# An encoder layer on one Trainium2 core: attention numerators turned, pattern weights through DRAM, pattern sums on GpSimd

## Chip, cores and metric

The kernel runs on one core of one Trainium2 chip. The metric is the device time of one execution in microseconds (us), lower is better. A difference of about 0.2% (5.6 us) is the smallest that a measurement of this kernel tells from no change.

## What is computed

One layer over 2048 tokens of width 1024, in float32: RMSNorm, one input projection to 4096 columns, a mixer of 8 attention heads (64 wide) beside 4 bidirectional HGRN2 heads (128 wide), an output projection with residual, then a mixture of 16 experts that each pick 256 tokens. The part that matters here is the attention:

```
for window, dilation in ((128, 1), (512, 4), (2048, 16)):     # three patterns
    m, den, num = dilated_window_attention(qh, kh, vh, window, dilation, slopes)
scale  = exp(m_all - max over patterns of m_all)
numer  = sum over patterns of scale * num                      # (S, heads, 64)
denom  = sum over patterns of scale * den
a_out  = numer / denom
x      = x + concat(a_out, hgrn_out) @ W_out
```

## The kernel before

The program is laid out by a scheduler that works with priorities: `first`, `feed`, `mixer`, `fill` are lanes, from most to least urgent, and the order on each engine is fixed when the program is built. The input projection runs as 16 units (`project`), each 8 token groups of 48 matmuls with 256 columns (L234 to L236); each weight is used as a high and a low half. Its weights come in 8 pieces (`prep`): a load into the ring `wraw` (5 buffers, L163, L166), then ScalarE makes the high half `whi` (L168) and VectorE the low half `wlo` (L169), both in rings of 11. So of the next unit's 8 pieces 3 can be made early, and 5 wait raw in `wraw`. The HGRN2 heads run in lane `mixer` beside the projections, then the 8 attention heads (`heads`, `att_head`) beside the last projections and beside half 1 of the output projection (`op_mm`, L799 to L801, HGRN columns), whose matmuls are in lane `fill`. After the heads `op_tile` does half 0 of the output projection (attention columns), the second norm and the router for 16 tiles of 128 tokens; then comes the routing search and the experts.

A head goes over four token groups g of 512. `four(pat, ...)` handles four units of 128 queries of one pattern in one or two `block`s. In a block TensorE forms the scores (L650, L651), VectorE adds the bias table and takes the minimum (L662, the scores are negated), ScalarE takes the exponential (L663), TensorE turns the result in four 128x128 transposes (L665), VectorE or ScalarE copies it to `eT` (L667, L669), and the numerator matmul (L674) has `eT` as the stationary operand, 128 columns wide, and the values as the moving one: 64 columns and a column of ones, which gives the denominator. float32 matmuls run as two passes, so each has two records in the trace. There are 8 x (32 + 32 + 16) = 640 numerator matmuls. Pattern 2 runs whole in g = 0. Numerators, denominators and minima (66 numbers a token) of patterns 0 and 2 go through DRAM (`num_d`, L698, L719, L726) into the token order of pattern 1. There VectorE makes the three weights (L732 to L738), scales (L739) and sums (L741, twice), and the result goes to `mix_d` in token rows (L742). `op_mm` reads a tile of `mix_d`, turns it on TensorE (L788), splits it in a high and a low half (L791, L792) and multiplies.

SyncE issues nearly all transfers from one queue, in order. GpSimd copies queries (`queries`, L621, L624), doubles keys (L547) and clears borders of `ex` (L653, L655).

Of the kernel before, what the change touches and what calls it, by code (L numbers as in the profile page):

```python
# [45 lines left out]
def encoder_layer(ctx, tc, x, norm1_w, w_in, q_norm_w, k_norm_w, lb_f, lb_b, o_norm_w, w_out,  # L46
# [26 lines left out]
    num_d = scratch("num_d", (2, 8, S, 66))  # L73
    mix_d = scratch("mix_d", (S, D))
# [86 lines left out]
    def prep(cols, kc):  # L161

        raw = ring.tile([128, 2, 128], F32, name="wraw", bufs=5)  # L163
# [8 lines left out]
    def evac_qk(u):  # L172

        def f(g, p):
# [5 lines left out]
            sq = ring.tile([128, 2, 256], F32, name="asq", bufs=1)  # L180
# [130 lines left out]
    def hg_head(p, T, h):  # L311
# [57 lines left out]
        for g in range(4):  # L369
# [125 lines left out]
            sp.dma_start(dram_ap(mix_d, a * D + 512 + h * 128, [[D, 128], [128 * D, 4], [1, 128]]), o)  # L495


    def att_setup(p):
        T = {}
        dl = p.tile([128, 512], F32, name="ex", bufs=4)  # L500
# [14 lines left out]
        T["wq"], T["wk"] = wq, wk  # L515
# [6 lines left out]

        T["vp"] = [p.tile([128, n, 65], F32, name=f"vp{i}", bufs=1) for i, n in enumerate((17, 20, 16))]
        for vp in T["vp"]:
            dve.memset(vp[:, :, 64:65], 1.0)

        for vp, n, step in ((T["vp"][0], 17, 16), (T["vp"][1], 20, 1)):
            for b in range(0, n, step):
                if step > 1 or b % 5 in (0, 4):
                    dve.memset(vp[:, b, :64], 0.0)  # L530
# [61 lines left out]
    def att_head(p, T, h):  # L592
# [48 lines left out]
        def block(pat, n0, qc, units, w, nst, pnum):  # L641
            vp = vps[pat]
# [27 lines left out]
            for j, un in enumerate(units):  # L670
                nb = len(un[3])
                for i, b in enumerate(un[3]):
                    c = j * w + i * 128
                    pe.matmul(pnum[:, n0 % 4 + j, :], eT[:, c:c + 128], vp[:, b, :], start=i == 0, stop=i == nb - 1)  # L674

        def four(pat, n4, nst):

            per = 4 if pat == 2 else 2
            pnum = pn([128, 512])[:, :260].rearrange("p (j c) -> p j c", j=4)
            qc = qs[:, n4 * 128:n4 * 128 + 512] if pat == 2 else qcs.pop((pat, n4 // 4))  # L680
            for n in range(n4, n4 + 4, per):
                block(pat, n, qc[:, n % 4 * 128:], [unit(pat, n + i) for i in range(per)], 512 // per, nst, pnum)
# [568 lines left out]
```

## Time and profile before

| | us |
|---|---|
| median of 3 runs (2775.2 to 2780.69) | 2777.16 |
| the profiled execution | 2778.25 |
| its span, first to last instruction | 2776.5 |
| TensorE busy | 2648.3 |
| VectorE busy | 1819.0 |
| ScalarE busy | 1428.0 |
| GpSimd busy | 228.4 |

The mean granted clock of TensorE is 0.977 of full speed. The attention heads lie from about 853 to 1447 us, `op_tile` from there to about 1577. A matmul's record is longer than its share of the engine, since matmuls are pipelined: what one costs is the distance from its start to the next start.

### The profile page before, as it was taken

The numbers are of one execution on the slowest core, as the hardware profiler recorded it, in microseconds if no ns is written. First come the engines' busy times: TensorE is split into PE (matmuls) and PEld (weight loads), VectorE is DVE, ScalarE is ACT, GpSimd is POOL, SyncE is SP. The second block draws the span as 40 slices with busy tenths as digits, with TensorE's granted clock in tenths as the row PEclk, the third lists the DMA queues.
The fourth block names the chain that finished last, engine by engine and source line by source line (L and its number), as shares of the span: only waits on it lengthen the run. The fifth ranks groups of instructions, "written<-read, shape, count | busy, mean of one in ns | idle before, by whom it ended". The sixth has DMA issues, their size and how long they took to land.

```text
span 2776.5 us, 59971 instructions
## 1 busy us (share of the span) xinstructions
PE 2648.3 (95%) x23494; PEld 2484.7 (89%) x23494; DVE 1819.0 (66%) x4562; ACT 1428.0 (51%) x2672; POOL 228.4 (8%) x413
## 2 busy tenths in 40 slices
PE   8999999999999999899889779999999999999998
PEld 8899899899999999788787579999999999999997
DVE  6538788888875577676766665555555555555553
ACT  6536667667655455443545434444444444444442
POOL 0000000000001222121210000000000000000000
PEclk9999999999999999999989879999999999999999
DMA  8887777777668665766538336666666666666663
GB/s 304 246 266 221 226 228 216 222 219 235 217 209 230 178 160 137 206 168 173 138 107 285 132 125 210 213 203 203 203 211 213 213 205 205 204 206 213 207 196 98
DMA packets 558859, 558.79 MB, mean 201 GB/s; under 512 B 144736, under 2 KB 509280, under 8 KB 558576
## 3 DMA queue, kind: packets, MB, share of 16 engines
q1 hardware_dynamic: 549040, 521.32, 59.9%
q0 software_dynamic: 9536, 33.64, 5.4%
q8 instruction: 185, 3.03, 0.5%
q14 instruction: 98, 0.80, 0.1%
HBM read 453.92 MB, written 100.93 MB: 200 GB/s over the span
## 4 chain that ended last, share of the span: by engine, by line
PE 78%; DMA 10%; DVE 7%; ACT 2%; SPq 1%; issue 1%; POOLq 0%; POOL 0%; DVEq 0%; ACTq 0%
PE mpg L1167 9%; PE mpg L1169 9%; PE mpg L1168 9%; PE pm L236 5%; PE pm L235 5%; PE pm L234 5%; PE mpy L1202 4%; PE mpy L1204 4%; PE mpy L1203 4%; PE pn L674 4%; DMA gz<-pf_d 3%; PE pm L801 2%; PE pm L799 2%; PE pb L665 2%; PE pm L800 2%; PE pa L650 1%
## 5 line engine op out<-in xcount | busy, mean ns | idle before, releaser
L1151 DVE TENSOR_TENSOR mlo<-mraw,mhi 128x1024 fp32r<-128x1024 f32 x384 | 470.0, 1224 | 461.1 <-ACT mhi L1150 460.6
L1150 ACT ACTIVATE mhi<-mraw 128x1024 fp32r<-128x1024 f32 x384 | 406.9, 1060 | 583.3 <-PE mpg L1168 402.0
L1167 PE MATMUL mpg<-xh,mhi 128*128 128x256 f32 x2048 | 579.7, 283 | 0.0
L1169 PE MATMUL mpg<-xh,mlo 128*128 128x256 f32 x2048 | 579.2, 283 | 0.0
L1168 PE MATMUL mpg<-xl,mhi 128*128 128x256 f32 x2048 | 576.6, 282 | 0.0
L1168 PEld LDWEIGHTS mpg<-xl,mhi 128*128 128x128 f32 x2048 | 387.6, 189 | 0.6
L1167 PEld LDWEIGHTS mpg<-xh,mhi 128*128 128x128 f32 x2048 | 386.6, 189 | 1.1 <-ACT xh L1123 0.4
L1169 PEld LDWEIGHTS mpg<-xh,mlo 128*128 128x128 f32 x2048 | 384.2, 188 | 0.0
L236 PE MATMUL pm<-whi,hlo 128*128 128x256 f32 x1280 | 365.1, 285 | 2.7 <-DMA hlo<-lo_d 2.7
L234 PE MATMUL pm<-whi,hth 128*128 128x256 f32 x1280 | 362.1, 283 | 5.6 <-ACT est L193 3.8
L235 PE MATMUL pm<-wlo,hth 128*128 128x256 f32 x1280 | 363.5, 284 | 1.2 <-DVE wlo L169 1.2
L234 PEld LDWEIGHTS pm<-whi,hth 128*128 128x128 f32 x1280 | 241.9, 189 | 6.8 <-ACT est L193 4.4
L236 PEld LDWEIGHTS pm<-whi,hlo 128*128 128x128 f32 x1280 | 241.9, 189 | 4.3 <-DMA hlo<-lo_d 3.9
L235 PEld LDWEIGHTS pm<-wlo,hth 128*128 128x128 f32 x1280 | 241.3, 189 | 2.4 <-DVE wlo L169 1.6
L234 PE MATMUL pm<-hth,whi 128*128 128x256 f32 x768 | 220.7, 288 | 4.8 <-ACT est L193 4.7
L236 PE MATMUL pm<-hth,wlo 128*128 128x256 f32 x768 | 218.2, 285 | 3.6 <-DVE wlo L169 3.6
L235 PE MATMUL pm<-hlo,whi 128*128 128x256 f32 x768 | 220.2, 287 | 1.1 <-DMA hlo<-lo_d 1.1
L1202 PE MATMUL mpy<-mhi,hh 128*128 128x512 f32 x512 | 205.9, 403 | 0.0
L1203 PE MATMUL mpy<-mlo,hh 128*128 128x512 f32 x512 | 203.9, 398 | 0.0
L1204 PE MATMUL mpy<-mhi,hl 128*128 128x512 f32 x512 | 202.9, 396 | 0.0
L674 PE MATMUL pn<-vp,eT 128*128 128x65 f32 x1280 | 162.0, 273 | 7.2 <-DVE eT L667 7.2
L674 PEld LDWEIGHTS pn<-vp,eT 128*128 128x128 f32 x1280 | 157.7, 194 | 10.6 <-DVE eT L667 9.5
(348 smaller groups left out, 5372.6 us busy)
## 6 DMA issues: line engine op xcount, KB each, us to landing
hlo<-lo_d SPq DMA_DIRECT2D x480, 256.0 KB, 4.2
mraw<-in_w_expert_gate_dram SPq DMA_DIRECT2D x64, 1024.0 KB, 5.5
mraw<-in_w_expert_up_dram SPq DMA_DIRECT2D x64, 1024.0 KB, 5.1
mraw<-in_w_expert_down_dram SPq DMA_DIRECT2D x64, 1024.0 KB, 5.1
wraw<-in_w_in_dram SPq DMA_DIRECT2D x128, 128.0 KB, 4.2
out_dram<-oxt SPq DMA_DIRECT2D x32, 512.0 KB, 3.9
pf_d<-est SPq DMA_DIRECT2D x96, 128.0 KB, 3.7
cb<-num_d SPq DMA_DIRECT2D x32, 264.0 KB, 3.7
```

Of the source, the lines that this page charges most:

```text
L234: pe.matmul(o, l[0], r[0], start=kc == 0, stop=False)
L235: pe.matmul(o, l[0], r[1], start=False, stop=False)
L236: pe.matmul(o, l[1], r[0], start=False, stop=kc == KC - 1)
L674: pe.matmul(pnum[:, n0 % 4 + j, :], eT[:, c:c + 128], vp[:, b, :], start=i == 0, stop=i == nb - 1)
L1150: act.activation(hi, src, AF.Copy)
L1151: dve.tensor_sub(lo, src, hi.bitcast(F32))
L1167: pe.matmul(o, hi[:, k, :], xh[:, k, :], start=k == 0, stop=False)
L1168: pe.matmul(o, hi[:, k, :], xl[:, k, :], start=False, stop=False)
L1169: pe.matmul(o, lo[:, k, :], xh[:, k, :], start=False, stop=k == KC - 1)
L1202: pe.matmul(o, hh[:, f, ts], hi[:, cs], start=f == 0, stop=False)
L1203: pe.matmul(o, hh[:, f, ts], lo[:, cs], start=False, stop=False)
L1204: pe.matmul(o, hl[:, f, ts], hi[:, cs], start=False, stop=f == KC - 1)
```

## The change

The numerators are formed turned: the values (64 columns) are stationary, `eT` moves. Two matmuls write the lower and the upper 64 rows of one PSUM tile, each with its half of the array's columns: for pattern 0 the halves are two units, with 128 moving columns; for patterns 1 and 2 they are two halves of one unit's queries, with 64. So there are 8 x 4 x (8 + 16 + 8) = 1024 numerator matmuls (L694 of the changed kernel) and always in the order lower half, upper half. All blocks of a `four` come before its numerators. The column of ones goes; the exponential's own sum (`accum_out`) gives the denominator, 384 times. Only denominators and minima (2 numbers a token) go through DRAM (`st_d`). `weights(g)` loads them back, VectorE makes the weights by the same operations as before, they go to `cw_d` and come back repeated over 64 rows (`wB`). `combine(g)` scales and sums on GpSimd in four operations and stores to `mixt_d`, which has features as rows. Both are called later than before: groups 0 to 2 later in the head, the rest in the next head. Pattern 2 moves from g = 0 to g = 1. Half 0 of `op_mm` reads `mixt_d` and needs no transposes. To make room the rings change: `wraw` 5 to 4, `ex` 4 to 3, `eT` 2 to 3, and `asq` shares the ring `est`.

```
-    num_d = scratch("num_d", (2, 8, S, 66))
-    mix_d = scratch("mix_d", (S, D))
+    st_d = scratch("st_d", (2, 8, S, 2))
+    cw_d = scratch("cw_d", (8, 3, S))
+    mixt_d = [scratch(f"mixt{g}_d", (512, 512)) for g in range(4)]
+    mix_d = scratch("mix_d", (S, 512))
...
-        raw = ring.tile([128, 2, 128], F32, name="wraw", bufs=5)
+        raw = ring.tile([128, 2, 128], F32, name="wraw", bufs=4)
...
-            sq = ring.tile([128, 2, 256], F32, name="asq", bufs=1)
+            sq = ring.tile([128, 2, 256], F32, name="est", bufs=2)
...
-        T["vp"] = [p.tile([128, n, 65], F32, name=f"vp{i}", bufs=1) for i, n in enumerate((17, 20, 16))]
-        for vp in T["vp"]:
-            dve.memset(vp[:, :, 64:65], 1.0)
+        T["vp"] = [p.tile([128, n, 64], F32, name=f"vp{i}", bufs=1) for i, n in enumerate((17, 20, 16))]
...
+        def block(pat, qc, units, w, st, on_act):
...
-            ex = p.tile([128, 512], F32, name="ex", bufs=4)
+            ex = p.tile([128, 512], F32, name="ex", bufs=3)
...
-            eT = p.tile([128, 512], F32, name="eT", bufs=2)
+            eT = p.tile([128, 512], F32, name="eT", bufs=3)
...
-                m = nst[:, n0 % 4 + j, 65:66]
+                m = st[:, j, 1:2]
...
-                act.activation(ex[:, c], ex[:, c], AF.Exp, bias=m, scale=-1.0)
+                act.activation(ex[:, c], ex[:, c], AF.Exp, bias=m, scale=-1.0, accum_out=st[:, j, 0:1])
...
-            if n0 % 8 < 6:
+            if on_act:
+                act.activation(eT, pT, AF.Copy)
+            else:
                 dve.tensor_copy(eT, pT)
+            return eT
+        def four(pat, n4, st, out):
...
+            pnum = pn([128, 512])[:, :256]
...
+            units = [unit(pat, n4 + i) for i in range(4)]
+            eTs = [block(pat, qc[:, i * 128:], units[i:i + per], w, st[:, i:i + per], (n4 + i) % 8 >= 6)
+                   for i in range(0, 4, per)]
+            if pat == 0:
+                todo = [[(hf, 2 * hf + u, slice(128 * u, 128 * u + 128)) for hf in range(2)] for u in range(2)]
             else:
-                act.activation(eT, pT, AF.Copy)
...
-                    pe.matmul(pnum[:, n0 % 4 + j, :], eT[:, c:c + 128], vp[:, b, :], start=i == 0, stop=i == nb - 1)
...
-            act.activation(nst[:, :, :65], pnum, AF.Copy)
+                todo = [[(hf, u, slice(64 * u, 64 * u + 64)) for hf in range(2)] for u in range(4)]
+            for pair in todo:
+                for i in range(len(units[0][3])):
+                    for hf, u, cols in pair:
+                        e = eTs[u // per][:, u % per * w + i * 128:u % per * w + i * 128 + 128]
+                        if pat == 1:
+                            e = e[:, 64 * hf:64 * hf + 64]
+                        elif pat == 2:
+                            e = e.rearrange("p (g f a) -> p g f a", g=4, f=2)[:, :, hf, :]
+                        pe.matmul(pnum[64 * hf:64 * hf + 64, cols], vp[:, units[u][3][i], :], e,
+                                  start=i == 0, stop=i == len(units[0][3]) - 1)
+            if pat == 0:
+                act.activation(out, pnum, AF.Copy)
+            elif pat == 1:
+                act.activation(out.rearrange("p (j r) -> p j r", r=4), pnum.rearrange("p (r j) -> p j r", r=4), AF.Copy)
+            else:
+                act.activation(out, pnum.rearrange("p (r a) -> p a r", r=4), AF.Copy)
...
+        def weights(g):
+            sg, wB, nt = grp[g]
+            for a in (0, 1):
+                sp.dma_start(sg[:, 2 * a].rearrange("p t c -> p (t c)"),
+                             dram_ap(st_d, ((a * 8 + h) * S + 512 * g) * 2, [[8, 128], [1, 8]]))
...
+            sp.dma_start(dram_ap(cw_d, h * 3 * S + 512 * g, [[4, 128], [S, 3], [1, 4]]), w)
+            wB = p.tile([128, 3, 256], F32, name="wB", bufs=2)
+            for hf in range(2):
+                sp.dma_start(wB[64 * hf:64 * hf + 64], dram_ap(cw_d, h * 3 * S + 512 * g + 256 * hf, [[0, 64], [S, 3], [1, 256]]))
...
+        def combine(g):
+            sg, wB, nt = grp.pop(g)
+            pool.tensor_mul(nt, nt, wB[:, :2])
+            pool.tensor_mul(wB[:, 2], wB[:, 2], n2[:, 256 * g:256 * g + 256])
+            pool.tensor_add(nt[:, 0], nt[:, 0], nt[:, 1])
+            pool.tensor_add(nt[:, 0], nt[:, 0], wB[:, 2])
+            for hf in range(2):
+                sp.dma_start(mixt_d[g][64 * h:64 * h + 64, 256 * hf:256 * hf + 256],
+                             nt[64 * hf:64 * hf + 64, 0])
...
+        def after(k):
+            for f in late.pop(k, []):
+                f()
         for g in range(4):
...
+            sg = p.tile([128, 3, 4, 2], F32, name="sg", bufs=4)
+            nt = p.tile([128, 2, 256], F32, name="nt", bufs=3)
...
+            st0 = p.tile([128, 4, 2], F32, name="st0", bufs=2)
...
-            four(0, 4 * g, n0)
...
-            sp.dma_start(dram_ap(num_d, h * S * 66 + row, [[66, 128], [128 * 66, 4], [1, 66]]), n0)
+            four(0, 4 * g, st0, nt[:, 0])
+            sp.dma_start(dram_ap(st_d, (h * S + 512 * g) * 2, [[2, 128], [256, 4], [1, 2]]), st0)
+            after(2 * g)
...
-            four(1, 4 * g, cb[:, 2])
+            four(1, 4 * g, sg[:, 1], nt[:, 1])
...
+            after(2 * g + 1)
...
+            if g == 1:
+                n2 = p.tile([128, S // 2], F32, name="n2", bufs=1)
+                st2 = p.tile([128, 16, 2], F32, name="st2", bufs=1)
                 for n4 in range(0, 16, 4):
-                    four(2, n4, n2[:, n4:n4 + 4, :])
-                sp.dma_start(dram_ap(num_d, (8 + h) * S * 66, [[16 * 66, 128], [66, 16], [1, 66]]), n2)
+                    four(2, n4, st2[:, n4:n4 + 4], n2.rearrange("p (a r) -> p a r", r=16)[:, :, n4:n4 + 4])
+                sp.dma_start(dram_ap(st_d, (8 + h) * S * 2, [[32, 128], [1, 32]]), st2.rearrange("p r c -> p (r c)"))
...
+                late[4] = [lambda: weights(0), lambda: weights(1)]
+                late[5] = [lambda: combine(0)]
+                late[6] = [lambda: combine(1), lambda: weights(2)]
...
-            dve.tensor_mul(cb[:, :, :, :64], cb[:, :, :, :64], w[:, :, :, None].to_broadcast([128, 3, 4, 64]))
-            for a in (0, 1):
-                dve.tensor_add(cb[:, 2, :, :64], cb[:, 2, :, :64], cb[:, a, :, :64])
-            sp.dma_start(dram_ap(mix_d, g * 512 * D + h * 64, [[4 * D, 128], [D, 4], [1, 64]]), cb[:, 2, :, :64])
+        late[0] = [lambda: weights(3)]
+        late[1] = [lambda: combine(2)]
+        late[2] = [lambda: combine(3)]
+        if h == 7:
+            for k in range(3):
+                after(k)
...
+    def op_mm(T, c, half, src):
...
             mt = op.tile([128, 512], F32, name="mx", bufs=2)
-            sp.dma_start(mt, mix_d[r, half * 512:(half + 1) * 512])
+            mtv = mt.rearrange("p (k t) -> p k t", k=4)
+            if half:
+                sp.dma_start(mt, mix_d[r, :])
+            else:
+                sp.dma_start(mtv, mixt_d[c // 4].rearrange("(k p) s -> p k s", p=128)[:, :, c % 4 * 128:c % 4 * 128 + 128])
...
+        if half:
+            with fill():
+                pt = pm()
+                for k in range(4):
+                    pe.transpose(pt[:, k * 128:(k + 1) * 128], mt[:, k * 128:(k + 1) * 128], ident)
+            mtv = pt.rearrange("p (k t) -> p k t", k=4)
         with feed():
...
+            act.activation(mh, mtv, AF.Copy)
+            dve.tensor_sub(ml, mtv, mh.bitcast(F32))
```

Three places show how the order moves. The first is SyncE's queue around the weights of one projection, number 8 of 0 to 15 (`wraw_8574` to `wraw_8616` are its 8 pieces, `wraw_9110` is the first of the next). Before, the eighth piece stands among the loads of the unit before:

```order
L218 DMA hlo_7031<-lo_d 128x2x256
L166 DMA wraw_8610<-in_w_in_dram 128x2x128
L199 DMA pt_d<-est_6908 128x2x256
L218 DMA hlo_7033<-lo_d 128x2x256
L218 DMA hlo_7035<-lo_d 128x2x256
L218 DMA hlo_7037<-lo_d 128x2x256
L218 DMA hlo_7091<-lo_d 128x2x256
L166 DMA wraw_8616<-in_w_in_dram 128x2x128
L199 DMA pt_d<-est_6968 128x2x256
L218 DMA hlo_7093<-lo_d 128x2x256
L218 DMA hlo_7095<-lo_d 128x2x256
```

And now, where the eighth piece (`wraw_8616`) stands 42 rows farther down, just ahead of the next unit's first:

```order
L201 DMA pt_d<-est_7268 128x2x256
L220 DMA hlo_8685<-lo_d 128x2x256
L220 DMA hlo_8687<-lo_d 128x2x256
L168 DMA wraw_8616<-in_w_in_dram 128x2x128
L220 DMA hlo_8689<-lo_d 128x2x256
L220 DMA hlo_8744<-lo_d 128x2x256
L168 DMA wraw_9110<-in_w_in_dram 128x2x128
L168 DMA wraw_9116<-in_w_in_dram 128x2x128
L201 DMA pt_d<-est_7328 128x2x256
L168 DMA wraw_9122<-in_w_in_dram 128x2x128
```

What moved: the eighth load is issued only when its own unit is about to begin.

The second is TensorE's order within the last head. Before (L650, L651 scores, L665 turns of `ex`, L674 numerators, L788 a turn of half 0):

```order
L650 MATMUL pa<-kh,qc 128x192
L651 MATMUL pa<-kl,qc 128x192
L650 MATMUL pa<-kh,qc 128x192
L651 MATMUL pa<-kl,qc 128x192
L674 MATMUL pn<-vp_12701,eT 128x65 x4
L665 MATMUL pb<-ident,ex 128x128 x4
L650 MATMUL pa<-kh,qc 128x192
L651 MATMUL pa<-kl,qc 128x192
L650 MATMUL pa<-kh,qc 128x192
L651 MATMUL pa<-kl,qc 128x192
L674 MATMUL pn<-vp_12701,eT 128x65 x4
L665 MATMUL pb<-ident,ex 128x128 x4
```

And now (L859 to L861 are out-projection matmuls of half 1, L664 turns, L694 numerators):

```order
L859 MATMUL pm<-woh,mh 128x512
L860 MATMUL pm<-wol,mh 128x512
L861 MATMUL pm<-woh,ml 128x512
L694 MATMUL pn<-eT,vp_12701 64x64 x8
L664 MATMUL pb<-ident,ex 128x128 x4
L694 MATMUL pn<-eT,vp_12700 64x128
L664 MATMUL pb<-ident,ex 128x128 x4
L859 MATMUL pm<-woh,mh 128x512
L860 MATMUL pm<-wol,mh 128x512
L861 MATMUL pm<-woh,ml 128x512
```

What moved: numerators come in runs of 8 with 64 or 128 moving columns, and out-projection matmuls stand between the blocks to the end; before, the last head and a half had none.

The third is GpSimd's order late in the first head: L732 to L735 are `combine`, L623 and L620 query copies, L654 a border that the last two blocks of the head need, L546 key copies.

```order
L623 COPY qc<-qs 128x512
L732 TENSOR_TENSOR nt<-nt,wB 128x512
L733 TENSOR_TENSOR wB<-wB,n_13071 128x256
L654 MEMSET ex 128x64 x2
L732 TENSOR_TENSOR nt<-nt,wB 128x512
L733 TENSOR_TENSOR wB<-wB,n_13071 128x256
L546 COPY x_13324<-x_13324 128x4x64
L608 COPY tab_15514<-tab_15514 128x128
L609 COPY tab_15514<-tab_15514 128x128
L734 TENSOR_TENSOR nt<-nt 128x256
L546 COPY x_13483<-x_13483 128x4x64
```

What moved: border and query copies now stand behind products that wait for `wB`; before, no such row was there.

## Rows read from the trace of the kernel before

**Rows 1.** Windows by stretch, all engines; the first row names the columns.
```profile
core 0: us, PE busy (x) PEld busy (x) DVE busy (x) ACT busy (x) POOL busy (x), PEclk, DMA share, GB/s
1191.00:1273.00 82.00, 81.60 (x560) 73.22 (x558) 57.61 (x193) 36.30 (x87) 17.96 (x44) 1.00 0.58 162
1345.00:1447.00 102.00, 86.31 (x634) 82.73 (x633) 69.80 (x254) 49.28 (x122) 18.90 (x46) 0.85 0.33 83
1447.00:1577.00 130.00, 123.98 (x828) 92.49 (x827) 83.16 (x274) 67.04 (x181) 7.01 (x9) 0.98 0.70 244
```

**Rows 2.** TensorE's waits, 853 to 1447 us: total us, times, longest.
```profile
PE pm L788 <- DMA mx<-mix_d: 9.7, 1, 9.7
```

**Rows 3.** Groups of TensorE, 1345 to 1447 us: count | busy us, mean ns | idle before.
```profile
L674 PE MATMUL pn<-vp,eT 128*128 128x65 f32 x280 | 38.4, 284 | 3.0 <-DVE eT L667 3.0
L650 PE MATMUL pa<-kh,qc 128*128 128x256 f32 (+1 forms) x54 | 17.7, 346 | 11.6 <-DVE cb L662 11.2 <-DVE n L662 0.4
L799 PE MATMUL pm<-woh,mh 128*128 128x512 f32 x12 | 4.9, 410 | 0.0
```

**Rows 4.** Timeline of TensorE without fill: start us, length, line, count.
```profile
1405.24 1.00 PE L674 MATMUL pn<-vp,eT 128*128 128x65 f32 x8
1406.08 0.60 PE L665 MATMUL pb<-ident,ex 128*128 128x128 f32 x4
...
1406.99 1.00 PE L674 MATMUL pn<-vp,eT 128*128 128x65 f32 x8
```

**Rows 5.** Timeline of TensorE, HGRN2: 32-column weights in four quarters of the array.
```profile
209.10 0.28 PE L236 MATMUL pm<-hth,wlo 128*128 128x256 f32 x1
209.22 0.28 PE L234 MATMUL pm<-hth,whi 128*128 128x256 f32 x1
209.43 0.40 PE L441 MATMUL pa<-gd 128*32 128x32 f32 x24
209.75 0.66 PE L335 MATMUL pb<-ident,gkd 128*128 128x128 f32 x4
```

**Rows 6.** Timeline of TensorE, router: the same with 128 moving columns.
```profile
1465.05 0.43 PE L836 MATMUL pn<-ht,wr 128*32 128x128 f32 x8
1465.41 0.66 PE L821 MATMUL pb<-ident,oxt 128*128 128x128 f32 x4
```

**Rows 7.** Timelines of VectorE, SyncE and TensorE where a projection unit begins.
```profile
72.44 2.08 DVE L169 SCALAR_TENSOR_TENSOR wlo<-wraw,w1c,whi 128x256 fp32r<-128x256 f32 x5 [2.83 <-ACT whi L168]
73.42 0.42 SPq L166 DMA_DIRECT2D wraw<-in_w_in_dram  x1
74.29 0.28 PE L234 MATMUL pm<-hth,whi 128*128 128x256 f32 x1
76.76 0.28 PE L234 MATMUL pm<-hth,whi 128*128 128x256 f32 x1
```

**Rows 8.** The page's transfers: KB each, median us from issue to landing.
```profile
wraw<-in_w_in_dram SPq DMA_DIRECT2D x128, 128.0 KB, 4.2
cb<-num_d SPq DMA_DIRECT2D x32, 264.0 KB, 3.7
```

**Rows 9.** Groups by line: VectorE, 853 to 1447 us, and ScalarE, whole span.
```profile
L739 DVE TENSOR_TENSOR cb<-cb,cw 128x768 f32<-128x768 f32 x32 | 31.9, 996 | 0.7
L741 DVE TENSOR_TENSOR cb<-cb 128x256 f32<-128x256 f32 x64 | 27.5, 429 | 0.8
L732 DVE TENSOR_REDUCE cm<-cb 128x4 f32<-128x12 f32 x32 | 5.5, 173 | 49.7 <-DMA cb<-num_d 49.5
L168 ACT ACTIVATE whi<-wraw,w1c 128x256 fp32r<-128x256 f32 x128 | 59.1, 500 | 35.8 <-DMA wraw<-in_w_in_dram 28.4 <-PE pm L236 4.3 <-PE pm L235 2.6
```

**Rows 10.** The line of the router's exponential: ns min/median/max.
```profile
L848 ACT ACTIVATION_READ_ACCUMULATOR olg<-pn,omx,osy x16: 190/191/201, 1463.4 to 1572.1; 128x1 f32 x16
```

**Rows 11.** Groups by line of GpSimd: two-operand products of 1024 and 256.
```profile
L856 POOL TENSOR_TENSOR h<-h,w 128x1024 f32<-128x1024 f32 x1 | 2.3, 2331 | 0.0
L1060 POOL TENSOR_TENSOR r<-afh,vals 128x256 f32<-128x256 f32 x1 | 0.8, 750 | 0.0
```

More of the change, by code (lines that the diff above doesn't have):

```diff
@@ L514, in att_setup @@
         dve.tensor_scalar(wq, wq, -0.125, None, op0=OP.mult)
-        T["wq"], T["wk"] = wq, wk
+        T["wq"], T["wk"], T["late"] = wq, wk, {}
         T["qs"] = p.tile([128, S], F32R, name="qs", bufs=1)
@@ L667, in block @@
                 dve.tensor_copy(eT, pT)
-            else:
-                act.activation(eT, pT, AF.Copy)
[L670 to L673, printed above, removed]
-                    pe.matmul(pnum[:, n0 % 4 + j, :], eT[:, c:c + 128], vp[:, b, :], start=i == 0, stop=i == nb - 1)
[L676 to L682, printed above, removed]
-            act.activation(nst[:, :, :65], pnum, AF.Copy)
@@ L687, in att_head @@
-        qcs = {(0, 0): queries(0, 0), (1, 0): queries(1, 0)}
+            return eT
+        def four(pat, n4, st, out):
+            per = 4 if pat == 2 else 2
+            w, vp = 512 // per, vps[pat]
+            pnum = pn([128, 512])[:, :256]
+            qc = qs[:, n4 * 128:n4 * 128 + 512] if pat == 2 else qcs.pop((pat, n4 // 4))
+            units = [unit(pat, n4 + i) for i in range(4)]
[3 more added lines that the diff above has]
+                todo = [[(hf, 2 * hf + u, slice(128 * u, 128 * u + 128)) for hf in range(2)] for u in range(2)]
+            else:
+                todo = [[(hf, u, slice(64 * u, 64 * u + 64)) for hf in range(2)] for u in range(4)]
[15 more added lines that the diff above has]
+                act.activation(out, pnum.rearrange("p (r a) -> p a r", r=4), AF.Copy)
@@ new lines, in att_head @@
+        qcs = {(0, 0): queries(0, 0), (1, 0): queries(1, 0)}
+        late = T["late"]
+        def weights(g):
[3 more added lines that the diff above has]
+                             dram_ap(st_d, ((a * 8 + h) * S + 512 * g) * 2, [[8, 128], [1, 8]]))
+            w = p.tile([128, 3, 4], F32, name="cw", bufs=2)
+            m8 = p.tile([128, 4], F32, name="cm", bufs=2)
+            d8 = p.tile([128, 4], F32, name="cd", bufs=2)
+            wd = p.tile([128, 3, 4], F32, name="cdd", bufs=2)
+            dve.tensor_reduce(m8, sg[:, :, :, 1].rearrange("p a t -> p t a"), axis=AX.X, op=OP.min)
+            dve.tensor_tensor(w, m8[:, None, :].to_broadcast([128, 3, 4]), sg[:, :, :, 1], op=OP.subtract)
+            act.activation(w, w, AF.Exp)
+            dve.tensor_mul(wd, w, sg[:, :, :, 0])
+            dve.tensor_reduce(d8, wd.rearrange("p a t -> p t a"), axis=AX.X, op=OP.add)
+            dve.reciprocal(d8, d8)
+            dve.tensor_mul(w, w, d8[:, None, :].to_broadcast([128, 3, 4]))
+            sp.dma_start(dram_ap(cw_d, h * 3 * S + 512 * g, [[4, 128], [S, 3], [1, 4]]), w)
+            wB = p.tile([128, 3, 256], F32, name="wB", bufs=2)
+            for hf in range(2):
+                sp.dma_start(wB[64 * hf:64 * hf + 64], dram_ap(cw_d, h * 3 * S + 512 * g + 256 * hf, [[0, 64], [S, 3], [1, 256]]))
+            grp[g] = sg, wB, nt
@@ L772, in op_weights @@
             dve.tensor_sub(T["wl"][:, k, :], raw, T["wh"][:, k, :].bitcast(F32))
-    def op_mm(T, c, half, src, bank):
+    def op_mm(T, c, half, src):
         op = T["op"]
@@ L784, in op_mm @@
             ml = op.tile([128, 4, 128], F32R, name="ml", bufs=2)
-        with fill():
-            pt = bank()
-            for k in range(4):
-                pe.transpose(pt[:, k * 128:(k + 1) * 128], mt[:, k * 128:(k + 1) * 128], ident)
+        if half:
[4 more added lines that the diff above has]
+            mtv = pt.rearrange("p (k t) -> p k t", k=4)
         with feed():
-            ptv = pt.rearrange("p (k t) -> p k t", k=4)
-            act.activation(mh, ptv, AF.Copy)
-            dve.tensor_sub(ml, ptv, mh.bitcast(F32))
+            act.activation(mh, mtv, AF.Copy)
+            dve.tensor_sub(ml, mtv, mh.bitcast(F32))
         for n in range(2):
@@ L916, in encoder_layer @@
     for c in range(NT):
-        op_mm(OT, c, 1, x[0], pm)
+        op_mm(OT, c, 1, x[0])
     with fill():
```

31 lines of the change are left out of this document (7 added, 24 removed).

## The prediction

> **What bounds the kernel now.** I read the windows by stretch first. The reader is to see that TensorE has no room in a head that runs beside other matmuls: 81.6 of 82 us are busy at full clock, while VectorE has 57.6, ScalarE 36.3 and GpSimd 18.0 [rows 1]. What shortens TensorE's work there shortens the head; work for the others is free as long as they keep up. The same view shows two other stretches. The last head and a half (1345 to 1447 us) keeps TensorE busy 86.3 of 102 us, at a mean granted clock of 0.85, so partly at the lower of its two levels, 1.2 instead of 2.4 GHz. `op_tile` (1447 to 1577 us) has TensorE busy 124 of 130 us. Next I read the groups of the head-and-a-half: the largest idle time stands before the scores and ends with VectorE's `cb` operation (L662), 11.2 us [rows 3]. So there the chain from one block to the next decides, since nothing else is left for TensorE. The waits of TensorE add one, 9.7 us for the first `mx` where the out-projection begins [rows 2].
>
> **Numerators (gain).** The busy time of a matmul is not its price. In the timeline without fill eight passes of L674 begin at 1405.24 and the next line at 1406.08 [rows 4]: 0.84 / 8 = 0.105 us a pass. 640 matmuls of two passes cost 1280 x 0.105 = 134.4 us. Afterwards two matmuls stand side by side in the two halves of the array; I call such a pair's pass a slot. Per `four` there are 8 slots with 128 moving columns (pattern 0), 16 with 64 (pattern 1) and 8 with 64 (pattern 2), each 32 times. No trace row shows halves, but two show quarters. The router's eight records with 128 columns, two in each quarter, take 0.36 us until the next line begins [rows 6], and HGRN2's group of 32-column passes takes 0.32 (32 are issued, the trace lists 24) [rows 5]. Both contain the change back to the whole array. Entering costs: the projection matmul ahead of the group takes 0.21 instead of 0.12 [rows 5], so 0.09 more. Taking 0.09 for leaving too, a slot is (0.36 - 0.09) / 2 = 0.135 with 128 columns and (0.32 - 0.09) / 8 = 0.029 with 32. I take 0.12 for 128 columns (a 256-column projection matmul has 0.12, so this is no better than a float32 pass at half its width), and half, 0.06, for 64, which is what doubling 0.029 gives. 32 x (8 x 0.12 + 16 x 0.06 + 8 x 0.06) = 76.8. The order shows 136 runs of numerators, since a `four`'s all stand together or nearly so: 136 x 2 x 0.09 = 24.5. Sum 101.3, **-33**. Bounds: no price for the change, -58; slots of 0.135 and 0.105 (a 64-column slot no cheaper than a pass of today), 34.6 + 80.6 + 24.5 = 139.7, +5.
>
> The Trainium skill ("TensorEngine Tiling (Array Packing)", Key Properties) says that a change of the tiling mode drains TensorE. The trace agrees, by 0.09 us a change [rows 5]; a longer drain after full-width matmuls would be the bound above.
>
> **Half 0 without turns (gain).** In the timeline four turns and four scores take 0.91 us [rows 4]; less 4 x 0.12 for the scores, a turn is 0.11. 16 tiles x 4 x 0.11 = **-7**, since `op_tile` is bound by TensorE [rows 1].
>
> **Fill in the last heads (gain).** Before, no out-projection matmul stands in the last head and a half; now the order puts them there, to the last block. The stretch has 280 numerator passes [rows 3], 35 blocks. A block's period is 1406.99 - 1405.24 = 1.75 us [rows 4], so 35 x 1.75 = 61 us; 35 out-projection matmuls (three lines like L799's 12) at twice the 0.12 of 256 columns are 8; 32 turns of the values, 4. Together 73 of 102 us: 29 are waits and low clock. If other matmuls fill them, their own time leaves the place where they stood: **-29**. That other place is a half-head in the middle which now runs with less beside it; with the 9.7 us at the change to the out-projection, which I keep, I call that even. Bounds: 0 and -39 (with the `mx` wait).
>
> **Weights ring of 4 (loss).** Before, an eighth piece waits raw in the ring when its unit begins. Now it is loaded only when piece 3 has been split, because the first three pieces have split buffers and the other five need raw ones. At a boundary VectorE ends five splits begun at 72.44 after 2.08 us, 0.42 each, so one is free at 72.86, and SyncE issues at 73.42 [rows 7]. Landing takes 4.2 us [rows 8], the high half 0.5 [rows 9]: 78.1. The unit began at 74.29 and uses its eighth piece at 76.76 [rows 7]. That is 1.4 us late; for the low half it is 1.8. I take 1.6 for the 13 units whose boundary has little else to run: **+21**. Bounds: 0 (the lanes put other matmuls in between) and 13 x 2.8 = 36 (two hops of the queue, 0.6 each, more).
>
> **Other engines (loss, mostly hidden).** ScalarE gets 384 accumulator reads of 0.19 us [rows 10], 73 us or 9.1 a head; a head has (1447 - 853) / 8 = 74 us, so its share of 44% [rows 1] becomes 56%, hidden behind TensorE. VectorE loses L739 and L741, 31.9 + 27.5 = 59.4 us [rows 9], and keeps the weights. GpSimd gets 32 combines: a product of 512 columns, half of 2.33, and three of 256 at 0.75 [rows 11], 3.4 us, 110 in all or 14 a head. Its share goes from 22% to 41%: room enough, if it doesn't wait. SyncE issues three small transfers more per group, in a queue whose DMA share is 0.58 [rows 1]. The nearest row for trouble is the present one, where `cb` is waited for 49.5 us in 32 places [rows 9] with TensorE hiding all of it; so I take little, 1.5 us a head, **+12**. Bounds: 0 and all that rival 2 counts.
>
> **Sum.** 2778.25 - 33 - 7 - 29 + 21 + 12 = 2742. The profiled execution is 1 us above the median of 2777.16 (2775.2 to 2780.69), so the forecast is the same for either.
>
> **Rivals.**
> 1. The ring and the other engines cost nothing: the scheduler finds other matmuls at the boundaries. 2742 - 33 = 2709. For it: HGRN2 work runs beside most units. Against: at the boundary shown, TensorE began its new unit at once, with the eighth piece due 2.5 us later [rows 7].
> 2. Slower: GpSimd's queue is held. `combine` waits for `wB`, which comes by a chain of four transfers (`st_d` out, `sg` in, `cw_d` out, `wB` in) where `cb` needed two. In the order, 27 copies of queries or clearings of borders, which the next blocks need, stand directly behind a row of `combine`. If `combine` is reached one transfer too early, 3.7 us [rows 8], each holds a block by it: 27 x 3.7 = 100. 2742 - 12 + 100 = 2830. It decides from (2778 - 2730) / 27 = 1.8 us a place. For it: `cb`, after two transfers, is already waited for by 49.5 / 32 = 1.5 us on average [rows 9]. Against: `weights` and `combine` are called some blocks after what they need, with at least a block's 4 us between.
> 3. The last heads stay bound by the chain. All blocks of a `four` now stand ahead of its numerators and `ex` has one buffer less, so the out-projection matmuls go in but the clock and the VectorE wait [rows 3] stay: 2742 + 29 = 2771.
> 4. The halves don't run side by side, and every slot costs twice: 2742 + 76.8 = 2819. Against: the quarters of rows 5 and 6 do. The Trainium skill (the same page, Restrictions) says that column tiling disables the fast weight load; that would be a way into this rival, and rows 5, with 32 loads and passes in 0.32 us, show no sign of it.
>
> **How the numbers follow.** Forecast 0.50 (own range 2715 to 2770), rival 1 0.20, rival 2 0.12, rival 3 0.13, rival 4 0.05. About 0.2%, 5.6 us, is what a measurement of this kernel tells from no change. Faster takes the forecast but for its upper 0.04, rival 1, and half of rival 3: 0.46 + 0.20 + 0.07 = 0.73, and a little of rival 2 where the hold is short, 0.75. Same takes 0.06, slower 0.19. The range leaves out the ends of rivals 2 and 4 and of rival 1: 2690 to 2800.
>
> **What would show it.** Right: eight numerator records of 64 columns follow at 0.03 us each, the distance to the next line 0.1 more at either side; the last head's clock is 1.00 and TensorE's idle before the scores gone; at a unit's eighth piece TensorE waits for `whi` or `wlo` by 1 to 2 us; `op_tile` is 7 us shorter. Wrong: GpSimd waits for `wB` with scores or exponentials waiting for GpSimd behind it (rival 2); the clock below 0.9 where fill now stands (rival 3); numerators at 0.06 us a record and no gain in a filled head (rival 4); ScalarE or VectorE over 90% busy in a head, which no case here has.

## The result and the profile after

The changed kernel takes 2845.03 us (2836.16 to 2853.88), 1.0239 of the kernel before (interval 1.0204 to 1.0275): 66 us slower, where 36 us faster was forecast, and outside the range. Differences below are those of such ratios, each to the kernel before measured beside it, times 2775 us.

Both kernels reach the first attention score at 848 us, the changed one with 108 more projection matmuls still to do (1042 against 934, by the traces). From the experts' first matmul (1623 us before, 1692 now) to the end of the span both take 1153 us. So all of the loss comes to light between. The windows of a filled head, one of the last heads, and the stretch behind the heads, columns as in [rows 1]:

```profile
core 0: us, PE busy (x) PEld busy (x) DVE busy (x) ACT busy (x) POOL busy (x), PEclk, DMA share, GB/s
961.00:1043.00 82.00, 65.26 (x652) 60.05 (x651) 37.31 (x148) 35.01 (x124) 26.85 (x55) 0.90 0.61 132
1334.00:1414.00 80.00, 70.42 (x599) 58.20 (x599) 44.33 (x157) 36.00 (x125) 24.72 (x45) 0.94 0.57 140
1450.00:1530.00 80.00, 61.17 (x279) 43.72 (x279) 33.38 (x106) 21.03 (x37) 14.35 (x26) 0.83 0.74 223
```

In [rows 1] a filled head had TensorE busy 81.6 of 82 us. Now it is 65.3 of 82, at a clock of 0.90. TensorE has less to do, as forecast, but the head isn't shorter: VectorE has 37 us of work where it had 58, ScalarE 35, GpSimd 27. None of these engines is full, so something waits. The numerators themselves came out as priced (start, length, line, count):

```profile
998.39 1.15 PE L694 MATMUL pn<-eT,vp 128*64 128x64 f32 x32
999.47 1.10 PE L664 MATMUL pb<-ident,ex 128*128 128x128 f32 x8
```

32 records, 16 slots of 64 columns, in 1.08 us until the next line: about 0.06 each and 0.1 for the change of mode, where 16 passes of the old kind took 1.68 [rows 4]. What the time goes to shows in one gap: SyncE's issues, then VectorE, then TensorE (a bracket is the idle time ahead and what ended it).

```profile
1002.94 0.50 SPq L711 DMA_DIRECT2D sg<-st_d  x1
...
1008.68 0.42 SPq L758 DMA_DIRECT2D st_d<-st  x1
...
1014.43 0.34 SPq L711 DMA_DIRECT2D sg<-st_d  x1
...
1002.88 0.43 DVE L606 SCALAR_TENSOR_TENSOR tab<-ad,tab 128x256 f32<-128x256 f32 x1
1017.75 0.17 DVE L717 TENSOR_REDUCE cm<-sg 128x4 f32<-128x12 f32 x1 [14.45 <-DMA sg<-st_d]
...
1008.22 0.28 PE L238 MATMUL pm<-whi,hlo 128*128 128x256 f32 x1
1019.00 0.58 PE L649 MATMUL pa<-kh,qc 128*128 128x256 f32 x1 [10.50 <-ACT kh L585]
```

VectorE has reached the weights (L717) in its fixed order and stands 14.45 us, from 1003.3. Until 1009.8 SyncE is busy with other issues, the store to `st_d` at 1008.68 among them. The next `sg` load waits for that store to land and goes out at 1014.43; nothing else is issued in between. Behind the weights, on VectorE, stand the minima and `eT` copies of the next blocks, and TensorE is idle for 10.5 us with scores (L649) waiting. The waits from 848 to 1450 us (total us, times, longest), two of the same kind in the kernel before (848 to 1447 us), and the transfers of the changed kernel (KB, median us to landing):

```profile
DVE cm L717 <- DMA sg<-st_d: 98.5, 22, 14.4
...
POOL nt L732 <- DMA wB<-cw_d: 105.5, 19, 15.7
...
SPq L711 <- DMA st_d<-st: 51.1, 21, 5.0
SPq L727 <- DMA cw_d<-cw: 20.4, 8, 5.1
```
```profile
DVE cm L732 <- DMA cb<-num_d: 49.5, 27, 3.5
...
SPq L726 <- DMA num_d<-n: 16.2, 12, 2.5
```
```profile
wB<-cw_d SPq DMA_DIRECT2D x60, 192.0 KB, 5.9
x<-qk_d SPq DMA_DIRECT2D x61, 128.0 KB, 4.9
...
sg<-st_d SPq DMA_DIRECT2D x63, 4.0 KB, 2.7
...
st_d<-st SPq DMA_DIRECT2D x32, 4.0 KB, 5.7
...
cw_d<-cw SPq DMA_DIRECT2D x31, 6.0 KB, 4.4
```

VectorE's wait of 49.5 us for `cb` has become one of 98.5 us in 22 places, up to 14.4. GpSimd waits 105.5 us for `wB`. SyncE itself stands 71.5 us for the trips' stores to land, where it stood 16.2. It also has more to issue: the trips and the stores of the results are 264 transfers (`st_d`, `sg`, `cw_d`, `wB`, `mixt_d`), where `num_d`, `cb` and `mix_d` were 104, so five more per group. Its issues from 848 to 1450 us take 379 us, where they took 277. The whole trip is 5.7 + 2.7 + 4.4 + 5.9 = 18.7 us, where `cb` took two transfers, the load 3.7 [rows 8].

### The profile page after: what moved, and what is told of

Read it like the earlier page. It is cut to its first block, busy times and chain, and to the rows that moved or that the text cites. A ratio compares the mean times of both kernels' runs of the same rounds, so it can differ in the third digit from the quotient of the medians.

```text
span 2845.8 us, 61997 instructions
## 1 busy us (share of the span) xinstructions
PE 2648.8 (93%) x24198; PEld 2440.1 (86%) x24198; DVE 1779.0 (63%) x4463; ACT 1461.0 (51%) x3056; POOL 329.7 (12%) x541
## 4 chain that ended last, share of the span: by engine, by line
PE 72%; DMA 14%; DVE 8%; ACT 2%; SPq 2%; issue 1%; POOL 0%; POOLq 0%; DVEq 0%; ACTq 0%
PE mpg L1227 9%; PE mpg L1229 9%; PE mpg L1228 9%; PE pm L237 5%; PE pm L238 5%; PE pm L236 5%; PE mpy L1262 4%; PE mpy L1264 4%; PE mpy L1263 4%; PE pn L694 2%; DMA gz<-pf_d 2%; PE pb L664 2%; PE pm L860 2%; PE pm L861 2%; PE pm L859 2%
## 5 line engine op out<-in xcount | busy, mean ns | idle before, releaser
L238 PEld LDWEIGHTS pm<-hth,wlo 128*128 128x128 f32 x768 | 145.7, 190 | 3.9 <-DVE wlo L171 3.8
L662 ACT ACTIVATE ex<-ex,st 128x256 f32<-128x256 f32 (+1 forms) x256 | 113.6, 446 | 68.4 <-DVE st L661 61.2
```

The lines of the kernel that those rows point to most:

```text
L238: pe.matmul(o, l[1], r[0], start=False, stop=kc == KC - 1)
```

## Experiments

Theories: 1, VectorE is held by `sg`; 2, GpSimd is held by `wB` (the prediction's second rival); 3, a block's chain bounds the heads; 4, several in-order queues hold and hide behind each other; 5, SyncE carries it.

**One trip cut, or all of it later.** Each edit below also lets the scheduler lay out the program anew. Cut runs leave out part of the computation, as each says. In e1 the weights use pattern 1's numbers alone:

```
-            for a in (0, 1):
-                sp.dma_start(sg[:, 2 * a]..., dram_ap(st_d, ...))
+            sg = sg[:, 1:2].to_broadcast([128, 3, 4, 2])
```

> The changed kernel without the two loads that bring denominators and minima of patterns 0 and 2 back (sg from st_d); the weights are formed from pattern 1's numbers alone, which are already on the chip, by the same operations; the stores, cw_d, wB and combine stay. Theory 1, VectorE is held: in the trace of the changed kernel TensorE's gaps in the heads that end with the first operation of the weights (L717) sum to some 60 us, so this kernel takes 2845 - 60 = 2785 us (2770 to 2800). Theory 2, GpSimd is held by wB: its waits for wB stay, so 2835 to 2845. Theory 3, the heads are bound by the chain of a block and the rest of the loss lies behind the heads: 2830 to 2845.

In e2 `combine` reads a constant tile:

```
-            pool.tensor_mul(nt, nt, wB[:, :2])
-            pool.tensor_mul(wB[:, 2], wB[:, 2], n2[...])
+            pool.tensor_mul(nt, nt, cB[:, :2])
+            pool.tensor_mul(n3, cB[:, 2], n2[...])
...
-                sp.dma_start(wB[64 * hf:64 * hf + 64], dram_ap(cw_d, ...))
```

> The changed kernel with combine reading a constant tile in place of wB, and without the loads of wB; weights and their loads of sg stay. Theory 1 (VectorE held): a gain of 0 to 15 us from a freer queue on SyncE, 2830 to 2845. Theory 2 (GpSimd held): the 106 us in 19 places that GpSimd waits for wB go, and most of the loss with them, 2745 to 2790. Theory 3 (chain): 2840 to 2845.

In e3 everything comes one `four` later, held by a dependence:

```
+            dve.tensor_copy(m8, T["held"])
...
-                late[4] = [weights(0), weights(1)]
+                late[5] = [weights(0), weights(1)]
```

> The changed kernel with the same work, but weights and combine called one four (two blocks, some 8 us) later, and held there by a copy that reads a minimum of the four before it. Theory 1 (VectorE held because the weights stand too early in its queue): sg has landed by then, as its chain of store and load takes 5.7 + 2.7 us at the median, so 2795 us (2770 to 2810). Theory 2 (GpSimd held): wB comes as late behind its call as before, 2840 to 2860. Theory 3: 2840 to 2850.

Measured: e1 1.0203 (1.0186 to 1.0221), e2 1.0097 (1.0081 to 1.0114), e3 1.0240 (1.0222 to 1.0257). So e1 gains some 10 us and its interval meets that of the change, e2 39, e3 nothing. The first theory alone doesn't carry the loss of 66 us, and the second gets 39 of it (its cut also takes 64 loads off SyncE). The waits of e1, then of e2, suggest why:

```profile
POOL nt L730 <- DMA wB<-cw_d: 113.4, 18, 14.2
...
SPq L725 <- DMA cw_d<-cw: 87.0, 24, 7.4
```
```profile
DVE cm L719 <- DMA sg<-st_d: 62.0, 21, 9.0
...
SPq L713 <- DMA st_d<-st: 88.5, 28, 6.5
```

Without `sg` the waits for `wB` (105.5 to 113.4) and SyncE's for `cw_d` (20.4 to 87.0) grow; without `wB` SyncE's for `st_d` do (51.1 to 88.5). One hold seems to have hidden the other.

**Both trips cut.** e6 is e1 and e2 together; e7 has the ring at five as well.

> The changed kernel with both round trips through DRAM cut: no loads of sg (weights from pattern 1's numbers alone) and no loads of wB (combine reads a constant tile); all stores, weights and combine's four operations stay. Theory 4, each trip holds another in-order queue and hides behind the other (VectorE by sg, GpSimd by wB, SyncE by both): more than the sum of the two single cuts, which gave 15 and 43 us, so 2760 us (2745 to 2775). Theory 3, a block's chain bounds the heads: the sum or less, 2787 to 2800.

> The same without round trips, and the ring of raw weights back at five buffers. The ring alone cost 17 us in the kernel before (2792 against 2775). Theory 4 with independent parts: 17 us less than without round trips alone, about 2743, and then 30 to 40 us below the kernel before: what numerators and half 0 save. If TensorE's saving never reached the path (theory 3): 2770 or more.

Measured: e6 0.9889 (0.9869 to 0.9909), e7 0.9848 (0.9828 to 0.9867). The two trips cost 3.5% or 97 us, twice the 49 of the single cuts. That price holds all that the 128 loads bring: their issues, their traffic, SyncE's waits for stores, and the waits of those who read. A filled head of e6, one of its last heads, and the stretch behind its heads:

```profile
948.00:1008.00 60.00, 60.00 (x650) 55.87 (x649) 38.53 (x154) 37.44 (x129) 26.01 (x54) 1.00 0.57 141
1253.00:1324.00 71.00, 71.00 (x620) 59.50 (x618) 44.72 (x152) 36.95 (x125) 25.01 (x45) 1.00 0.50 135
1356.00:1423.00 67.00, 54.17 (x260) 38.64 (x257) 32.79 (x102) 20.30 (x33) 7.94 (x15) 0.90 0.78 248
```

TensorE is busy 60.0 of 60 and 71.0 of 71 us at full clock: theory 3 falls too. The stretch behind the heads is not full (54 of 67): there the rest of the out-projection's half 1 runs with nothing beside it.

**The prediction's other terms.** e5 is the kernel before with `bufs=4` for `wraw`, e10 is e6 with

```
-                for i in range(len(units[0][3])):
+                for i in [i for i in range(nb)] * 2:
```

> The kernel before with four instead of five buffers for raw projection weights, nothing else. The prediction's term: 2778 + 21 = 2799 us (range 0 to 36 more). From the changed kernel's trace: both kernels reach the first attention score at 848 us, but the changed one has some 108 projection matmuls of 0.12 us left over, so 2778 + 13 = 2791. If other matmuls fill the boundaries: 2778 to 2783.

> The kernel without round trips (2742 us) with every numerator matmul issued twice in a row of its sums (the second pass overwrites the first). It prices the numerators where they stand. If TensorE bounds the heads and the prediction's price holds: the 76.8 us of slots once more, the changes of mode being shared, so 2742 + 77 = 2819 (2805 to 2845). If the chain of a block bounds the heads, so that TensorE has room: 2742 to 2780.

Measured: e5 1.0057 (1.0040 to 1.0074), 16 us, and e6 to e7 11 us back. In e5's trace 124 more projection matmuls than before are left at the first score (1058 against 934), 124 x 0.12 = 15 us. Half of that shows in one gap of TensorE, which the kernel before doesn't have:

```profile
711.51 0.58 PE L234 MATMUL pm<-whi,hth 128*128 128x256 f32 x1 [7.64 <-ACT ast L176]
```

There a projection matmul waits for ScalarE's copy of an earlier result (`ast`, L176), which in ScalarE's order stands behind high halves of weights; the first of them waited 1.91 us for its load. The gap stands in the change and in e6 too (7.72 and 7.59 us), and not in e7. The waits for `whi` and `wlo` themselves, up to 848 us, grow only from 6.6 to 10.7 us, the longest 2.0.

e10 is 1.0118 (1.0089 to 1.0147), 64 us above e6 for 77 us of slots: most of a numerator's price is on the path.

**Which queue.** In e8 the loads read an input tensor, so they wait for no store. In e9 each hop is held by one more `four`, and in e11 only the readers are; both have `sg` at 5, `nt` at 4 and `hlo` at 8. In e12 the copies of queries and the borders move to VectorE.

```
-                             dram_ap(st_d, ...)        (e8, and cw_d alike)
+                             dram_ap(x, ...)
...
-                late[4] = [weights(0), weights(1)]      (e11)
+                late[4] = [fetch(0), fetch(1)]
+                late[5] = [weights(0), weights(1), fetch(2)]
...
-                pool.tensor_copy(qc..., v...)           (e12)
+                dve.tensor_copy(qc..., v...)
```

> The changed kernel with the loads of sg and wB of the same shapes and sizes, but from an input tensor that nothing writes, so that they wait for no store; the stores stay. It tells the waits for a store's landing (SyncE stands in them, 51 us for st_d and 20 for cw_d) from the loads themselves. If the store-to-load dependence is the cost: within 15 us of the kernel without round trips, 2760 to 2780. If the loads themselves are (64 loads of 192 KB repeated over 64 rows, 5.8 us each): 2820 to 2845.

> All of the changed kernel's work, with each hop of the trips held back by one more four (some 8 us): loads of sg, then weights, then loads of wB, then combine, each tied by a small copy or addition of zero to the minima of a later four; one more buffer for nt and sg, one less for hlo. Theory 4 (a hop's landing is waited for because the hop behind it stands too early in an in-order queue): 2780 (2765 to 2800). If it isn't the order but the transfers themselves, or if holding costs as much as waiting: 2820 to 2850.

> All of the changed kernel's work; sg is loaded as early as before, the weights are held one four later, combine two fours after its weights, each by a dependence on a later four's minima; one more buffer for nt and sg, one less for hlo. If the engines' places behind the loads are the cost (theory 4): 2775 (2760 to 2800), since every landing has 8 us or more. If SyncE's own waits, with all other loads behind them, carry most of it: 2815 to 2840.

> The changed kernel with the copies of queries and the clearing of borders on VectorE instead of GpSimd, so that no block waits for what stands behind combine; VectorE gets some 5 us a head more. If GpSimd's place is the cost (the prediction's second rival, as it was put there): as without wB, 2800 to 2815. Theory 4 (the hold moves to VectorE and SyncE): 2825 to 2850.

Measured: e8 1.0183 (1.0163 to 1.0203), e9 1.0177 (1.0156 to 1.0198), e11 1.0211 (1.0182 to 1.0240), e12 1.0313 (1.0279 to 1.0347). 16, 17 and 8 us back, and 21 lost; e11's 8 us are not clear of noise, as its interval meets that of the change. All three missed the range that I had favoured and fell into the other. For e8 that other range stood for the loads themselves as the cost, not for their waits: no load of the trips has a store to wait for, and yet e8 is 82 us above e6. Its waits, the end of one stretch of SyncE's issues, and the rows of VectorE and TensorE there:

```profile
DVE cm L717 <- DMA sg<-in_x_dram: 97.1, 12, 16.4
...
1323.06 2.43 SPq L727 DMA_DIRECT2D wB<-in_x_dram  x2
1325.53 1.07 SPq L711 DMA_DIRECT2D sg<-in_x_dram  x2
...
1314.08 0.68 DVE L863 TENSOR_TENSOR oxt<-oxt,pm 128x512 f32<-128x512 f32 x1
1331.17 0.17 DVE L717 TENSOR_REDUCE cm<-sg 128x4 f32<-128x12 f32 x1 [16.41 <-DMA sg<-in_x_dram]
...
1332.69 1.12 PE L694 MATMUL pn<-eT,vp 128*64 128x64 f32 x16 [11.22 <-DVE eT L668]
```

SyncE's waits for stores ahead of these loads fall from 71.5 to 5 us, but VectorE still waits 97.1 us for `sg`. From 1314.8, when VectorE begins to stand, to 1326.2, when the second of these `sg` loads goes out, SyncE issues 17 other transfers, 9.2 us of its time. In each of the seven waits over 8 us the load goes out 4 to 11 us after VectorE began to wait, behind 8 to 17 other transfers. So the loads are late by their place in SyncE's queue too, not only by the stores. What e12 shows is that freeing the copies behind `combine` brings nothing that its added work on VectorE doesn't eat.

In e14 the loads of `sg` and `wB` go, waits and all, into tiles that nothing reads:

```
+            sgd = p.tile([128, 2, 8], F32, name="sgd", bufs=4)
-                sp.dma_start(sg[:, 2 * a]..., dram_ap(st_d, ...))
+                sp.dma_start(sgd[:, a], dram_ap(st_d, ...))
...
-            wB = p.tile([128, 3, 256], F32, name="wB", bufs=2)
+            wB = p.tile([128, 3, 256], F32, name="wB", bufs=1)
```

> As without round trips (2742 us: weights from pattern 1's numbers, combine from a constant tile), but the loads of sg and wB are issued all the same, into tiles that nothing reads; they wait on SyncE for the landing of their stores as before. It parts the 103 us: what is left above 2742 is SyncE's standing in the waits, with the other loads behind, and the traffic; what is gone is VectorE, ScalarE and GpSimd waiting for the data. If SyncE carries the cost: 2800 to 2840. If the engines that read the data carry it: 2745 to 2770.

Measured: 1.0370 (1.0353 to 1.0388), 133 us above e6 with no reader at all. SyncE's waits and TensorE's longest (848 to 1460 us), then one stretch of SyncE's issues with GpSimd's row beside it, and one of ScalarE's from another place:

```profile
SPq L730 <- DMA cw_d<-cw: 70.9, 25, 5.1
SPq L714 <- DMA st_d<-st: 57.7, 21, 6.1
...
PE pa L651 <- POOL qc L622: 47.4, 6, 13.6
...
1061.97 0.56 SPq L786 DMA_DIRECT2D st_d<-st  x1
1064.97 1.30 SPq L714 DMA_DIRECT2D sgd<-st_d  x3
...
1067.35 0.42 SPq L762 DMA_DIRECT2D st_d<-st  x1
1071.73 0.81 SPq L714 DMA_DIRECT2D sgd<-st_d  x2
1072.63 0.38 SPq L540 DMA_DIRECT2D x<-qk_d  x1
...
1075.01 0.40 POOL L548 COPY x<-x 128x256 f32<-128x256 f32 x1 [24.54 <-DMA x<-qk_d]
...
1117.15 0.51 ACT L170 ACTIVATE whi<-wraw,w1c 128x256 fp32r<-128x256 f32 x1 [20.77 <-DMA wraw<-in_w_in_dram]
```

SyncE stands 128.6 us for stores. The load of `x` (the next head's keys) goes out at 1072.63, behind two such waits and the issues between, so GpSimd has stood 24.54 us in its order with copies of queries behind, for which TensorE's scores wait (47.4 us in all); at 1117 ScalarE has stood 20.77 us for `wraw`, with exponentials behind. So a fuller and longer held queue on SyncE can cost this much with no reader. The run doesn't part its causes, the 128 loads with their traffic and the standing; and SyncE stands longer here than in the change, 128.6 against 71.5 us, and `wB` has one buffer.

**The loads and their waits taken off SyncE, all work kept.** In e17 GpSimd issues the dependent transfers:

```
-                sp.dma_start(sg[:, 2 * a]...
+                pool.dma_start(sg[:, 2 * a]...
...
-                sp.dma_start(wB[64 * hf:64 * hf + 64], ...
+                pool.dma_start(wB[64 * hf:64 * hf + 64], ...
...
-                sp.dma_start(mixt_d[g]...
+                pool.dma_start(mixt_d[g]...
```

e15 adds e12's edit, e16 e11's as well.

> The changed kernel with only the loads of sg and wB and the stores to mixt_d issued by GpSimd; queries and borders stay on GpSimd, behind its waits. Theory 5 with the hold moved: SyncE's part goes, GpSimd's grows, 2820 to 2850. If SyncE alone matters and GpSimd has slack: 2770 to 2790. If GpSimd's place behind the waits is the dearest: above 2860.

> All of the changed kernel's work; the loads of sg and wB and the stores to mixt_d are issued by GpSimd into its own queue, and the copies of queries and the borders are on VectorE, so that behind those waits there stand only key copies and combine. The dead loads (2879 us with nobody reading) point to SyncE's standing in waits for stores, 128 us of them, with key and weight loads behind. Theory 5, SyncE carries the cost: it now waits for no store of the trips, so 2785 us (2760 to 2810; VectorE's added copies cost 15, as measured). If the reading engines carry it: 2850 to 2880, as VectorE still stands at sg and GpSimd's issues are added.

> The same, with weights held one four later and combine two fours after them, one more buffer for nt and sg, one less for hlo. Theory 5: SyncE is free and VectorE finds sg landed, 2765 us (2745 to 2790), level with the kernel before or below it. If the reading engines or GpSimd's own queue carry the cost: 2820 to 2870.

Measured: e17 1.0087 (1.0053 to 1.0120), e15 1.0210 (1.0179 to 1.0240), e16 1.0070 (1.0046 to 1.0095). e17 gets 42 of the 97 us back, though GpSimd now does the waiting:

```profile
POOL sg L711 <- DMA st_d<-st: 90.5, 27, 7.2
...
DVE cm L717 <- DMA sg<-st_d: 49.7, 13, 6.5
```

GpSimd stands 90.5 us for `st_d`, where SyncE stood 51.1, but SyncE's other loads no longer stand behind that, and VectorE waits 49.7 instead of 98.5 us for `sg`. SyncE is also rid of 192 of the run's 1827 transfers; its issues from 848 to 1450 us take 283 us, as in the kernel before (277). So e17 takes the waits and the issues off SyncE together and doesn't part them. e12's edit costs 34 us here too (e15 against e17). On top of it slack for the readers counts: e16 is 39 us below e15, where the same edit gave 8 to the change. e2, e12, e14, e15 and e17 came out outside every range that I had set for them. In e13 the weights of two groups are formed together, 16 times instead of 32 (of the transfers only the loads of `sg` become fewer, 32 instead of 64), with `nt` at 4, `hlo` at 8 and a single `wB` of double length; e18 is e17 with e11's edit and five `wraw`, e19 is e17 with e13's and five; both have one `tab1` and `hlo` at 8.

```
-                late[4] = [weights(0), weights(1)]      (e13; sg, w, wB twice as long)
+                late[4] = [weights(0)]
...
-        late[0] = [weights(3)]
+        late[0] = [weights(2)]
```

> All of the changed kernel's work, but the weights of two groups are formed together: 16 chains of store, load, weights, store, load instead of 32, with twice the content each; one more buffer for nt, one less for hlo, a single wB of double length. If each chain costs a hold wherever it stands (103 us for 32, so 3.2 each): about 2845 - 50 = 2795 (2780 to 2815). If the cost goes with bytes and transfers, or with the gaps that the schedule leaves, rather than with the number of chains: 2825 to 2850.

> All of the changed kernel's work: the loads of sg and wB and the stores to mixt_d in GpSimd's queue (alone: -45), weights held one four and combine two fours later (alone: -14), and five buffers for raw weights (-11), paid for with one hlo and one tab1 buffer less. If the three add, 2845 - 70 = 2775 (2760 to 2790). If slack only helps where SyncE is free, so that the parts more than add: 2745 to 2760. If the shared buffers cost: above 2795.

> All of the changed kernel's work: the same queue for the loads and stores (-45), the weights of two groups formed together (alone: -25), and five buffers for raw weights (-11), with one hlo and one tab1 buffer less. If the parts add: 2845 - 81 = 2764 (2750 to 2780), some 10 us under the kernel before. If pairs crowd GpSimd's queue: 2785 or more.

Measured: e13 1.0166 (1.0149 to 1.0183), e18 1.0036 (1.0019 to 1.0052), e19 0.9935 (0.9913 to 0.9957): 2756.58 us, with the whole computation, 18 us below the kernel before and 84 below the change. Pairs alone gave 20 us (e13). e18 is only 14 us below e17, of which the ring alone gave 11 (e6 to e7): without e12's edit slack adds little, so whether it helps is not settled.

## Why the prediction was wrong

- **The step that failed** is "Other engines (loss, mostly hidden)", with its +12. There I gave SyncE's added transfers no price, counted three more per group where there are five, and took the present wait for `cb`, hidden behind TensorE, as the measure (27 waits, by the view above, not 32). The trips cost 97 us (e6). The old trip had two transfers and the longest wait for it was 3.5 us; the new one has four, one behind the other, and its loads reach the readers up to 14.4 us late, because they stand behind other issues in SyncE's queue and, in part, because each waits there for a store. Taking away the waits for stores alone gave 16 us (e8), taking loads, waits and result stores off SyncE 42 (e17), leaving out the loads 97. The sum without this step and with the ring is 2742 - 12 = 2730; e6 measured 2742. That is in part luck, as the terms below err both ways.
- **The second rival** had the size (+100) and the root, a trip of four transfers reached too early, but put the place on GpSimd's copies and gave it 0.12. Cutting `wB` gave 39 us, freeing the copies nothing net (e12). The largest part that one edit with all work kept gave back lies on SyncE's queue (42 us, e17), which I had named only as a count of issues. I had looked for what stands behind `combine` and not for what stands ahead of and behind a load in SyncE's order.
- **Numerators, -33:** right. The order's 2048 passes take the 101 us that I summed: in e7's trace the starts of numerators and what follows them add up to 101.1 us.
- **Ring, +21:** 16 in the kernel before (e5), 11 in the changed one (e6 to e7). The size came out near, but not by 13 waits of 1.6 us for an eighth piece: the waits for `whi` and `wlo` grew by 4 us in e5, and one gap of 7.64 us behind ScalarE's copy, which I hadn't looked for, makes up half.
- **Half 0, -7, and fill in the last heads, -29:** the out-projection's matmuls did go into the last heads, and in e6 these run full. But the out-projection begins later (in e7 at 1196 us, against 1129 before), and in e7 120 of the 384 matmuls of half 1 come behind the heads, in a stretch with TensorE busy 49 of 61 us. I had called this exchange even. e7, with the ring back and no trips, is 42 us below the kernel before, where the terms give 33 + 7 + 29 = 69; I put the missing 27 down to this stretch, by the windows; that is not shown, as no run changes it alone, nor half 0's turns by themselves.
- **Rivals 1, 3 and 4:** out. The ring cost 11 to 16 us and the trips 97. Without trips the heads run full at clock 1.00 (e6), and the halves do run side by side (16 slots in 1.08 us).
- **Open:** how the trips' cost parts between SyncE's issues and its waits for stores (no run took away the issues alone), and how the 55 us between e17 and e6 part between VectorE's and GpSimd's waits (no run cut one of the two with SyncE free). Pairs and the ring gave 42 us on top of e17 (e19), which leaves 24 to e7.

## What to carry to other kernels

Before a result goes through DRAM and back, ask what its transfers do to the queue that issues them: how many they add, which of its loads wait there for a store, what other transfers stand ahead of those loads, and which stand behind. The price is paid by readers whose data comes late and, as e14 shows, by engines that never touch the trip. Taking away the waits for stores alone gave little here (16 us); moving the dependent transfers to the queue of an engine with room gave 42, and with the weights formed for two groups at a time and the ring restored 84. And if one cut gives little, cut all trips together before dismissing them: 10 and 39 us alone were 97 together.

## What was not expected of the hardware

A store of 4 KB in 8-byte pieces (`st_d`) took 5.7 us to land in the change and 5.2 in e6, longer than the stores of 132 KB in 264-byte pieces that it replaced (3.3 by the same view of the kernel before): less content made the store no quicker. The Trainium skill ("DMA: Bandwidth & Descriptors", Specifications) says that pieces under 512 bytes are read, modified and written. That alone doesn't tell these apart, since both are under it, and pattern 2's store in 128-byte pieces took 2.4 us in the change and 4.6 in e6; no run here changed the size of the pieces alone.
